# A hybrid decoder layer on one core: v of the last four heads in its own place, banks evacuated first, half of w_out split during attention

## The chip, the core and the metric

The kernel runs on one core of one Trainium2 chip. The core has five engines that work side by side, each through its own instructions in their order: TensorE (PE in the profile, PEld its weight loads), VectorE (DVE), ScalarE (ACT), GpSimd (POOL) and SyncE (SP), which here only issues DMAs. They wait for one another through semaphores. The metric is the device time of one launch in microseconds. Before the change the median of three runs was 2474.42 us (2474.41 to 2474.8).

## The reference

One layer over 2048 tokens of width 1024, in float32, with four RMS norms:

```
a   = RMSNorm(x)
mix = [ mLSTM, 4 heads || causal attention, 8 heads ](a) @ w_out
x   = x + RMSNorm(mix)
x   = x + RMSNorm( relu(RMSNorm(x) @ w_up)^2 @ w_down )
```

The input projection w_in gives q and k of the mLSTM (which go through a causal convolution of four taps and silu), its v, output gates and scalar gates, and two latents, c_q and c_kv, with one rotary key. The latents are normed and multiplied into q, k and v of the eight attention heads (64 plain and 32 rotary dimensions; v has 64). The mLSTM is computed in chunks with a carried state.

## The kernel before, in words

**Precision.** Nearly every operand is split in two: a high part rounded to the fast matmul type (ACT, a cast) and the low part that is left (DVE or POOL, a subtraction). A product is three matmuls, high by high, high by low, low by high: `mm3`, lines 220 to 222, the lines under which most matmuls stand in the profile.

**The order.** The instructions are not written in the order in which they run. Each step is handed to a planner (`Plan`, method `op`) with an engine, a cost in nanoseconds, the steps that it comes after, a key, the buffers ("rings") that it takes and those that it frees. `Plan.run` simulates the engines: on each it takes the step that can start first, and among those that can start at once the one with the smallest key; it calls the step, which emits its instructions, and so fixes the order on every engine. `kA(b, t)` = -400 + (123 b + t)/1.8 turns a place in block b of the projections into a key; in attention a key is a place in the sequence of score blocks, from 0 at the first. The chip then runs each engine's list in that order, and an instruction that is not ready holds back what stands behind it.

**Projections (four blocks of 512 tokens).** Per block: 16 units of 24 matmuls (`unit`, `values`), which accumulate in one of two PSUM banks, the ring "mm". A bank is free when its contents are evacuated: in `conv` by DVE into "raw" (L1051), in `gates` by DVE (L1131), in `values` by ACT into "vext" (L1104). From the latents come "kp", "vp", "qp" and "rp" (`operands`), in the same two banks; ACT copies the high part (`hi`, L727, L778), DVE the raw value (`raw`, L730, L781), POOL makes the low part. These evacuations have the key of their place, the products' 5 more (`PQ`). Beside them DVE runs the convolutions' taps (L1063), the rotation of the rotary key (`rotate`, L876 to 888, key `kA(b, KROT)`), the latents' gains (L675, key `kA(b, LGAIN)`), weight splits (L457) and the gates' scalar chain; `chunk` is the mLSTM (scores, exponentials, numerators L1186 and L1187, state, root, L1243 transposes, store "hT<-ho"). q, k and v of attention go to DRAM (qkd, qrd, krd, vd). In the last block the value units come at the end (`LASTLINE`).

**The switch to attention.** Memory is a stack on each side. On the left lie the convolutions' and latents' buffers (pool e2); on the right those of the chunks (b1, b2) and above them x and w (xp, wp). `switch1` closes e2; `switch2`, after the last unit, closes x and w and opens on the left the first operand set (QK[0]: q and k of one head, high and low, 97 rows by 4 by 2048) with the mask; `switch3`, after the last chunk, opens on the right v (16 tiles by 4 heads by 129 columns), the second operand set QK[1] and the buffers of attention. A tile's first write waits for the tiles whose memory it takes.

**Attention (8 heads, 4 query blocks each).** `maxima` finds each query's largest score ("m" products L1527, reductions on DVE into "mp" L1532 and L1534). `step` handles one block of 128 keys by up to 512 queries: three matmuls into S (three banks), two exponentials on ACT (L1591, L1595), the low part pl on DVE or, in one of five, on POOL (L1599), and the products with v into o (L1612, L1610, L1615). `out_rows` copies o away: ACT and DVE into "ot" (L1682, L1685), DVE into "ou" (L1689), POOL adds (L1692), SP stores "hT<-ot" (L1695) and the sums. "ot", "ou" and the two o banks have one buffer each. `load_v` (L1500) loads v for heads 0 to 3, and for heads 4 to 7 into the same tile, each pair of key tiles after its last product of head 3.

**Output projection and MLP.** `matrix(k)` loads 128 rows of w_out ("wor", ring "wr", two buffers), and ACT (L1822) and DVE (L1825) split two halves of them into tiles w0 to w11 or "wx". The pool `work` that holds these is opened by `left`, after all maxima and after head 6. `group` multiplies ("op") and adds the residual; the MLP follows with w_up and w_down in the same w tiles.

Of the kernel before, what the change touches and what calls it, by code (L numbers as in the profile page):

```python
# [10 lines left out]
F32 = mybir.dt.float32  # L11
# [28 lines left out]
EARLY = ()  # L40
LOL = 20.0
# [10 lines left out]
VLEAD = 0.0  # L52
# [9 lines left out]
CHUNK = 0.0  # L62
# [4 lines left out]
LGAIN = 30.0  # L67
# [3 lines left out]
KROT = 90.0  # L71
# [45 lines left out]
class Plan:  # L117
# [23 lines left out]
    def run(self):  # L141
# [70 lines left out]
def trunk(ctx: ExitStack, tc: tile.TileContext, x, xT, pos, wu, wout, wup, wdn, cols, rows, consts, edge, out, dbg=None):  # L212
# [486 lines left out]
    def operands(b, t, o_c, held):  # L699
# [25 lines left out]
        def two_parts(nm, n, q, last, first, key, store, kb):  # L725
# [36 lines left out]
        for n in range(4):  # L762
# [7 lines left out]
            def vevac(q, last, first, n=n, key=key):  # L770
# [16 lines left out]
                h = pl.op("Activation", 600, hi, [g, last], key + PQ, free=[("mm", first)])  # L787
                o_staged[b].append(g)
                d = pl.op("DVE", 690, raw, [g, last], key + PQ, free=[("mm", first)])
# [250 lines left out]
    def conv(b, j):  # L1040
# [36 lines left out]
        e = pl.op("DVE", 660, evac, [r, u["op"], o_rsbc[b]], key, free=[("mm", u["head"]), ("rsbc", o_rsbc[b])])  # L1077
# [11 lines left out]
    def values(b):  # L1089
# [3 lines left out]
        def one(c):  # L1093
# [22 lines left out]
            o_vx[b, c] = pl.op("Activation", 650, evac, [last, rs_x[b]["op"], *war], kA(b, TIME[b][5 + c] + 2), free=[("mm", head)])  # L1116
# [4 lines left out]
    def gates(b, h):  # L1121
# [9 lines left out]
        o = pl.op("DVE", 660, lambda: vec.tensor_tensor(g, u["p"], rsbc[b], ALU.mult), [u["op"], o_rsbc[b], *war], key, free=[("mm", u["head"]), ("rsbc", o_rsbc[b])])  # L1131
# [243 lines left out]
    a2 = av = ar2 = pq = pS = po = V = onecol = maskneg = maskb = identb = None  # L1375
# [9 lines left out]
    def switch1():  # L1385

        s_e.close()

    def switch2():

        nonlocal a2, maskneg, pq
        s_x.close()
# [4 lines left out]
        pq = pp(pc, "pq", 1)  # L1397
        pm.append(pp(pc, "pm", 2))

    def switch3():  # L1400

        nonlocal av, ar2, pS, po, V, maskb, identb, onecol
        s_b.close()
        av = sb(pa, "av", 1, "right")
# [8 lines left out]
        V = av.tile([P, NT, 4, 129], F32R, tag="V", name="V")  # L1413
# [4 lines left out]
    o_s1 = pl.op("X", 0, switch1, pl.groups["e2"], -KEYA)  # L1418
    o_s2 = pl.op("X", 0, switch2, unit_ops + [o_s1], -KEYA)
    o_s3 = pl.op("X", 0, switch3, pl.groups["in"] + [o_s2], -KEYA)  # L1420
    pl.group = "prep"
    for name, bufs, when in (
        ("q", 1, o_s2), ("m", 2, o_s2), ("S", SB_, o_s3), ("o0", 1, o_s3), ("o1", 1, o_s3), ("t", TB_, o_s3), ("th", 1, o_s3), ("tl", 1, o_s3), ("ph", HB_, o_s3), ("p", 1, o_s3), ("pl", LB_, o_s3), ("ot", 1, o_s3), ("ou", 1, o_s3),
        ("mp", 4, o_s2), ("mx", 2, o_s2), ("rsm", 2, o_s3),
    ):
        pl.ring(name, bufs, when)

    o_mask = pl.op("SP", 500, lambda: dma(maskneg, consts[:, K_MASK : K_MASK + 512]), [o_s2], key=-99, kb=256)
    o_const = {}
    for s in (0, "v", 1):  # L1430

        def fill(s=s):
            if s == "v":
                pool.memset(f32(V[:, :, :, 128:129]), 1.0)
# [7 lines left out]
        o_const[s] = pl.op("Pool" if s == "v" else "SP", 490 if s == "v" else 1500, fill, [o_s3 if s else o_s2], key=-99 if s == 0 else -50, kb=0 if s == "v" else 24)  # L1442
# [37 lines left out]
    def rotary_keys(s, b, key):  # L1480
        bs = slice(b * TB, (b + 1) * TB)
        o_kr[s, b] = pl.op("SP", 500, lambda: dma(f32(QK[s][64:96, 2:4, bs]), krd[:, :, bs]), [*o_krds[b], o_s3 if s else o_s2], key, kb=128)
# [1205 lines left out]
```

## Time and profile before

| | us |
|---|---|
| median of 3 runs | 2474.42 |
| the profiled execution | 2470.98 |
| its span, first to last instruction | 2469.2 |
| last matmul of a value unit | 539.2 |
| first product of attention with v ("o") | 564.4 |
| first product of the output projection ("op") | 1028.0 |

The span is the time from the first to the last instruction of that execution; 1.8 us of the execution lie outside it. The page gives the busy time of each engine; the granted clock says at what share of its full speed TensorE was let run (1.00 or, after idle stretches, 0.50), and a matmul at half clock counts as busy all the same. A row of the timeline gives the start, the duration, the engine, the line, the operation, the tile that is written and those that are read, and in brackets how long the engine had been idle and what ended that. A row of the waits gives the waiting engine, tile and line, whom it waited for, and total, number and longest of these waits. A row of the stages gives, per stretch, its length, busy time and number of instructions of PE, PEld, DVE, ACT and POOL, the granted clock, the DMA engines' busy share and the GB/s. SPq rows are DMAs being issued.

### The profile page before, as it was taken

To read this page: it belongs to the slowest core of one execution; us is meant where nothing else is said; L and a number is where in the kernel's file an instruction comes from. 1 tells how busy PE (TensorE), PEld (TensorE's weight loads), DVE (VectorE), ACT (ScalarE), POOL (GpSimd) and SP (SyncE) were. 2 spreads that over 40 slices of the span, in tenths; PEclk is the share of its full clock that TensorE was granted. 3 is DMA by queue.
4 is the path that set the end of the run, shared out by engine and by line. 5 is a ranking of instruction groups with operands and counts; after the bars stand their busy time and mean duration, and the time that the engine had idled before them with its cause. 6 is when DMAs were issued, how large, how long until landed. Compare 5 with 4: busy or idle time off the path is not lost.

```text
span 2469.2 us, 34097 instructions
## 1 busy us (share of the span) xinstructions
PE 2391.8 (97%) x10915; PEld 1920.1 (78%) x10915; DVE 1769.7 (72%) x3160; ACT 1359.8 (55%) x2638; POOL 811.1 (33%) x705
## 2 busy tenths in 40 slices
PE   8899999999999899999999999999999999999997
PEld 6677787677777677678888888888888888888885
DVE  6767565647887788754876677866676688786888
ACT  5545454436777777643666666756565343343454
POOL 3434333336878788522100000000000233232334
PEclk9999999999999999999999999999999999999999
DMA  6796969766325220466777798756664545445459
GB/s 239 231 331 212 342 220 334 225 194 143 69 57 109 66 53 10 136 194 226 258 213 218 227 284 249 218 160 194 195 194 141 165 136 165 136 138 167 131 164 244
DMA packets 345564, 456.02 MB, mean 185 GB/s; under 512 B 35324, under 2 KB 227848, under 8 KB 345384
## 3 DMA queue, kind: packets, MB, share of 16 engines
q1 hardware_dynamic: 341448, 446.98, 58.4%
q0 software_dynamic: 3936, 6.87, 1.7%
q8 instruction: 86, 1.41, 0.3%
q14 instruction: 94, 0.77, 0.1%
HBM read 302.79 MB, written 153.05 MB: 185 GB/s over the span
## 4 chain that ended last, share of the span: by engine, by line
PE 78%; DVE 7%; DMA 6%; issue 3%; POOL 2%; ACT 2%; SPq 1%; DVEq 0%; POOLq 0%; ACTq 0%
PE S L220 2%; PE o L1612 2%; PE mm L220 2%; PE o L1615 2%; PE S L221 2%; PE S L222 2%; PE mm L222 2%; PE mm L221 2%; PE m L1527 2%; PE op L220 1%; PE op L222 1%; PE op L221 1%; DMA hr<-hd 1%; PE mv L220 1%; PE mv L221 1%
## 5 line engine op out<-in xcount | busy, mean ns | idle before, releaser
L2499 POOL TENSOR_TENSOR y<-vd_0X,y 128x512 f32<-128x512 f32 x7 | 11.4, 1622 | 724.9 <-ACT vd_0X L2496 706.9
L1591 ACT ACTIVATE ph<-S 128x512 fp32r<-128x512 f32 (+1 forms) x320 | 170.2, 532 | 97.2 <-PE S L222 28.9
L1626 POOL TENSOR_TENSOR t<-t,ph 128x512 f32<-128x512 f32 (+1 forms) x192 | 210.3, 1096 | 16.5 <-ACT ph L1591 6.2
L2411 ACT CAST hh<-hr 128x512 fp32r<-128x512 f32 (+1 forms) x208 | 116.7, 567 | 168.2 <-DMA hr<-hd 37.3
L1599 DVE TENSOR_TENSOR pl<-S,ph 128x512 fp32r<-128x512 f32 (+3 forms) x272 | 157.0, 590 | 30.9 <-ACT S L1595 28.9
L220 PE MATMUL mm<-xh,wh 128*128 128x512 f32 x384 | 159.6, 416 | 11.5 <-ACT wh L452 7.7
L2416 DVE TENSOR_TENSOR hl<-hr,hh 128x512 fp32r<-128x512 f32 (+1 forms) x208 | 130.2, 635 | 36.6 <-ACT hh L2411 28.9
L221 PE MATMUL mm<-xl,wh 128*128 128x512 f32 x384 | 151.2, 394 | 2.7 <-DVE xl L382 2.7
L222 PE MATMUL mm<-xh,wl 128*128 128x512 f32 x384 | 151.2, 394 | 0.5 <-DVE wl L457 0.5
L1532 DVE TENSOR_REDUCE mp<-m 128x1 f32<-128x512 f32 x192 | 128.9, 682 | 29.3 <-PE m L1527 29.2
L1595 ACT ACTIVATE S<-S 128x512 f32<-128x512 f32 (+3 forms) x272 | 140.9, 518 | 0.3
L220 PE MATMUL S<-QK 97*128 97x512 f32 (+1 forms) x320 | 123.7, 386 | 5.9 <-DVE pl L1599 4.7
L1612 PE MATMUL o<-ph,V 128*128 128x512 f32 (+1 forms) x320 | 122.0, 382 | 7.5 <-DVE ot L1685 7.5
L221 PE MATMUL S<-QK 97*128 97x512 f32 (+1 forms) x320 | 118.6, 371 | 0.0
L1527 PE MATMUL m<-QK 96*128 96x512 f32 (+3 forms) x320 | 114.9, 405 | 3.4 <-DVE mp L1532 1.8
L222 PE MATMUL S<-QK 97*128 97x512 f32 (+1 forms) x320 | 118.1, 369 | 0.0
L1615 PE MATMUL o<-pl,V 128*65 128x512 f32 (+1 forms) x320 | 115.8, 364 | 1.2 <-DVE pl L1599 0.9
L2250 ACT ACTIVATE t<-t 128x512 f32<-128x512 f32 x96 | 60.6, 631 | 79.5 <-DVE t L2245 79.1
L220 PE MATMUL op<-wo,hh 128*128 128x512 f32 x256 | 101.9, 398 | 2.5 <-DVE x L1920 1.2
L222 PE MATMUL op<-wo,hl 128*128 128x512 f32 x256 | 100.5, 393 | 0.0
L221 PE MATMUL op<-wo,hh 128*128 128x512 f32 x256 | 100.5, 393 | 0.0
L220 PEld LDWEIGHTS mm<-xh,wh 128*128 128x128 f32 x384 | 73.0, 190 | 32.5 <-ACT wh L452 8.0
(6441 smaller groups left out, 7564.0 us busy)
## 6 DMA issues: line engine op xcount, KB each, us to landing
hr<-hd SPq DMA_DIRECT2D x100, 448.0 KB
wr<-in_wu_dram SPq DMA_DIRECT2D x71, 512.0 KB
hd<-t SPq DMA_DIRECT2D x128, 256.0 KB
hd<-ts SPq DMA_DIRECT2D x96, 256.0 KB
wl<-wparts SPq DMA_DIRECT2D x45, 512.0 KB
QK<-qkd SPq DMA_DIRECT2D x32, 512.0 KB
xt<-in_x_dram SPq DMA_DIRECT2D x28, 512.0 KB
xf<-xd SPq DMA_DIRECT2D x40, 256.0 KB
```

Source lines behind the costliest of these rows:

```text
L220: pe.matmul(o, ah, bh, start=start, stop=False)
L221: pe.matmul(o, ah, bl, start=False, stop=False)
L222: pe.matmul(o, al, bh, start=False, stop=stop)
L1527: pe.matmul(ps[:, :n], Qh[s][0:96, q0 : q0 + P], Kh[s][0:96, kb * TB : kb * TB + n], start=True, stop=True)
L1532: vec.tensor_reduce(mp["t"][:, j, kb : kb + 1], ps, axis=AX.X, op=ALU.max)
L1591: act.activation(t["h"][:, :w], t["S"][:, :w], AF.Exp)
L1595: act.activation(t["p"][:, :w], t["S"][:, :w], AF.Exp)
L1599: (pool if by_pool else vec).tensor_tensor(t["l"][:, :w], t["p"][:, :w], f32(t["h"][:, :w]), ALU.subtract)
L1612: pe.matmul(o0, v[:, 0:128], t["h"][:, :w], start=start, stop=stop)
L1615: pe.matmul(o1, v[:, 64:129], t["l"][:, :w], start=start, stop=stop)
L1626: pool.tensor_tensor(to, to, hv, ALU.add)
L2416: vec.tensor_tensor(t["l", m][:, :w], t["r", m][:, :w], f32(t["h", m][:, :w]), ALU.subtract)
```

## The change

Six things at once, all through the planner or the places of tiles:

- **Evacuations first.** `EV = 8` is taken from the keys of what frees an "mm" bank: the products' `hi` and `raw`, `conv`'s and `gates`' evacuation on DVE, `values`' on ACT. `PQ` goes from 5 to 0.
- **Other keys.** The rotation (`KROT` 90 to 50) and the latents' gains (`LGAIN` 30 to 20) come earlier, the chunks 2 later (`CHUNK`), v's loads 6 earlier (`VLEAD`).
- **First operand set at switch1.** QK[0], the mask and one maxima bank are opened when e2 closes, and their loads (mask, edge rows, rotary keys, q and k) are allowed from then on.
- **v twice.** `V[0]` (heads 0 to 3) is opened on the left by `switch2`, `V[1]` (heads 4 to 7) on the right by `switch3`; the loads of V[1] no longer wait for head 3.
- **w_out.** A pool work0 with the tiles w0 to w7 and "wr" is opened on the right by `switch3`. The first four of eight row blocks of w_out are loaded and split from then on, with keys at 0.6, 0.7, 0.8 and 0.9 of attention's length; the others as before.
- **"Z".** The steps that switch pools move from the planner's engine "X" to "Z", whose steps take effect at the end of what they follow, without the planner's latency. `EARLY` is empty, so the lines that would move maxima forward do nothing.

```diff
-VLEAD = 0.0
+VLEAD = 6.0
-CHUNK = 0.0
+CHUNK = 2.0
-LGAIN = 30.0
+LGAIN = 20.0
-KROT = 90.0
+KROT = 50.0
+W0 = 8
+W0K = 0.6
+W0S = 0.1
+EV = 8.0
-PQ = 5.0
+PQ = 0.0
...
-            if ops[d][0] == "X" or ops[d][0] == eng and eng != "SP":
+            if ops[d][0] in "XZ" or eng == "Z" or ops[d][0] == eng and eng != "SP":
...
-            h = pl.op("Activation", 570, hi, [g, last], key, free=[("mm", first)])
+            h = pl.op("Activation", 570, hi, [g, last], key - EV, free=[("mm", first)])
-            d = pl.op("DVE", 690, raw, [g, last], key, free=[("mm", first)])
+            d = pl.op("DVE", 690, raw, [g, last], key - EV, free=[("mm", first)])
...
-        e = pl.op("DVE", 660, evac, [r, u["op"], o_rsbc[b]], key, free=[("mm", u["head"]), ("rsbc", o_rsbc[b])])
+        e = pl.op("DVE", 660, evac, [r, u["op"], o_rsbc[b]], key - EV, free=[("mm", u["head"]), ("rsbc", o_rsbc[b])])
...
     def switch1():
 
+        nonlocal a2, maskneg, pq
         s_e.close()
-
-    def switch2():
-
-        nonlocal a2, maskneg, pq
-        s_x.close()
         a2 = sb(pc, "a2", 2)
         a1 = sb(pc, "a1", 1)
         set_tiles(a1, 0)
         maskneg = a1.tile([P, 512], F32, tag="maskneg", name="maskneg")
         pq = pp(pc, "pq", 1)
+
+    def switch2():
+
+        s_x.close()
         pm.append(pp(pc, "pm", 2))
+        V[0] = sb(pc, "a3", 1).tile([P, NT, 4, 129], F32R, tag="V0", name="V0")
 
     def switch3():
 
         s_b.close()
+        pools["work0"] = sb(ctx, "work0", 1, "right")
         av = sb(pa, "av", 1, "right")
...
-        V = av.tile([P, NT, 4, 129], F32R, tag="V", name="V")
+        V[1] = av.tile([P, NT, 4, 129], F32R, tag="V1", name="V1")
...
-        war = [o_pv[index[3, qb, kt]] for qb in range(NB) for kt in (t, t + 1) if (3, qb, kt) in index] if g else [o_const["v"]]
-        o_v[g, t] = [pl.op("SP", 1000, load, [o_vd[t], o_vd[t + 1], o_s3] + war, key, kb=512)]
+        o_v[g, t] = [pl.op("SP", 1000, load, [o_vd[t], o_vd[t + 1], *([o_s3, o_const["v"]] if g else [o_s2, o_const["v0"]])], key, kb=512)]
...
+    def wpool(ring):
+        return "work0" if int(ring[1:]) < W0 else "work" if int(ring[1:]) < WB else "w2"
...
     def wrow(name):
-        return pools["work"].tile([P, DM], F32, tag="wr", name=name, bufs=2)
+        return pools["work0"].tile([P, DM], F32, tag="wr", name=name, bufs=2)
...
-        key = END + 2 * k
-        a = pl.op("SP", 500, load, [o_left], key, take=("wr",), kb=512)
+        early = 2 * k + 1 < W0
+        key = END * (W0K + W0S * k) if early else END + 2 * k
+        a = pl.op("SP", 500, load, [o_s3 if early else o_left], key, take=("wr",), kb=512)
```

More of the change, by code (lines that the diff above doesn't have):

```diff
@@ L40 @@
 EARLY = ()
+EKEY = -165.0
+EGAP = 1.5
 LOL = 20.0
@@ L786, in vevac @@
                 g = pl.op("X", 0, place, [last], key + PQ, take=("sg",))
-                h = pl.op("Activation", 600, hi, [g, last], key + PQ, free=[("mm", first)])
+                h = pl.op("Activation", 600, hi, [g, last], key + PQ - EV, free=[("mm", first)])
                 o_staged[b].append(g)
-                d = pl.op("DVE", 690, raw, [g, last], key + PQ, free=[("mm", first)])
+                d = pl.op("DVE", 690, raw, [g, last], key + PQ - EV, free=[("mm", first)])
                 d = pl.op("Pool", 1300, lo, [h, d], key + PQ)
@@ L1115, in one @@
             war = o_chunk.get((b - 1, c), {}).get("v", [o_fill2])
-            o_vx[b, c] = pl.op("Activation", 650, evac, [last, rs_x[b]["op"], *war], kA(b, TIME[b][5 + c] + 2), free=[("mm", head)])
+            o_vx[b, c] = pl.op("Activation", 650, evac, [last, rs_x[b]["op"], *war], kA(b, TIME[b][5 + c] + 2) - EV, free=[("mm", head)])
         for c in range(4):
@@ L1130, in gates @@
         war = [x for c in range(4) for x in o_chunk.get((b - 1, c), {}).get("gate", [])]
-        o = pl.op("DVE", 660, lambda: vec.tensor_tensor(g, u["p"], rsbc[b], ALU.mult), [u["op"], o_rsbc[b], *war], key, free=[("mm", u["head"]), ("rsbc", o_rsbc[b])])
+        o = pl.op("DVE", 660, lambda: vec.tensor_tensor(g, u["p"], rsbc[b], ALU.mult), [u["op"], o_rsbc[b], *war], key - EV, free=[("mm", u["head"]), ("rsbc", o_rsbc[b])])
         o = pl.op("Activation", 590, lambda: act.activation(g, g, AF.Tanh, scale=0.5), [o], key)
@@ L1372, in trunk @@
             chunk(b, c)
-    a2 = av = ar2 = pq = pS = po = V = onecol = maskneg = maskb = identb = None
+    V = {}
+    pools = {}
+    a2 = av = ar2 = pq = pS = po = onecol = maskneg = maskb = identb = None
     pm = []
@@ L1433, in fill @@
             if s == "v":
-                pool.memset(f32(V[:, :, :, 128:129]), 1.0)
+                pool.memset(f32(V[1][:, :, :, 128:129]), 1.0)
                 pool.memset(f32(onecol[:, 0:64]), 0.0)
@@ L1440, in fill @@
                     pool.dma_start(z[s][96:97, :], edge[1:2])
[L1442 removed]
+        o_const[s] = pl.op("Pool" if s == "v" else "SP", 490 if s == "v" else 1500, fill, [o_s3 if s else o_s1], key=EKEY - 30 if s == 0 else -50, kb=0 if s == "v" else 24)
     blocks, first, start_of = [], {}, {}
@@ L1481, in rotary_keys @@
         bs = slice(b * TB, (b + 1) * TB)
-        o_kr[s, b] = pl.op("SP", 500, lambda: dma(f32(QK[s][64:96, 2:4, bs]), krd[:, :, bs]), [*o_krds[b], o_s3 if s else o_s2], key, kb=128)
+        o_kr[s, b] = pl.op("SP", 500, lambda: dma(f32(QK[s][64:96, 2:4, bs]), krd[:, :, bs]), [*o_krds[b], o_s3 if s else o_s1], key, kb=128)
     def load_qk(h, b, key):
@@ L1731, in trunk @@
         run += c
+    early = [x for x in EARLY for _ in range(4 * x[1] + 4)]
+    for i, x in enumerate(early):
+        keys[(*x, "m")][early[:i].count(x)] = EKEY + EGAP * i
     for s in range(2):
         for b in range(NB):
-            rotary_keys(s, b, -40 if s else -90 + b)
+            rotary_keys(s, b, -40 if s else EKEY - 30 + b)
     for h in range(NH):
@@ L1759, in trunk @@
     po1, po2, pA, pX, pB = (ExitStack() for _ in range(5))
-    pools = {}
     pl.group = "switch"
@@ L1768, in left @@
         pools["pmA"] = pp(pA, "pmA", 1)
-    o_left = pl.op("X", 0, left, pl.groups["prep"] + [o_pv[index[6, qb, kt]] for qb in range(NB) for kt in range(4 * qb + 4)], END)
+    o_left = pl.op("Z", 0, left, pl.groups["prep"] + [o_pv[index[6, qb, kt]] for qb in range(NB) for kt in range(4 * qb + 4)], END)
     for o in o_tail:
@@ L1775, in trunk @@
         pl.ring(name, bufs)
+    def wpool(ring):
+        return "work0" if int(ring[1:]) < W0 else "work" if int(ring[1:]) < WB else "w2"
     def wtile(name, ring):
-        where = "o1" if ring == "wx" else "work" if int(ring[1:]) < WB else "w2"
+        where = "o1" if ring == "wx" else wpool(ring)
         return pools[where].tile([P, 2, TB], F32R, tag=ring, name=name, bufs=4 if ring == "wx" else 1)
     def wrow(name):
-        return pools["work"].tile([P, DM], F32, tag="wr", name=name, bufs=2)
+        return pools["work0"].tile([P, DM], F32, tag="wr", name=name, bufs=2)
     def srow(name):
@@ L2105, in open_b @@
         pools["xb"] = sb(pX, "xb", 1, "right")
-    o_open = pl.op("X", 0, open_b, pl.groups["out"] + [o_openA], UP)
+    o_open = pl.op("Z", 0, open_b, pl.groups["out"] + [o_openA], UP)
     for z in ("Y0", "Y1", "Z0", "Z1"):
@@ L2528, in load @@
         def load():
-            q["x"] = pools["work" if int(ring[1:]) < WB else "w2"].tile([P, DM], F32, tag=ring, name=f"fx{ti}")
+            q["x"] = pools[wpool(ring)].tile([P, DM], F32, tag=ring, name=f"fx{ti}")
             dma(q["x"], x1d[ti * P : (ti + 1) * P, :])
```

29 lines of the change are left out of this document (15 added, 14 removed).

## The prediction

> **What bounds the kernel now.** I read the page first: shares of busy time and the chain that ended last.
>
> ```profile
> span 2469.2 us, 34097 instructions
> PE 2391.8 (97%) x10915; PEld 1920.1 (78%) x10915; DVE 1769.7 (72%) x3160; ACT 1359.8 (55%) x2638; POOL 811.1 (33%) x705
> PE 78%; DVE 7%; DMA 6%; issue 3%; POOL 2%; ACT 2%; SPq 1%; DVEq 0%; POOLq 0%; ACTq 0%
> ```
>
> TensorE is the bound. The change takes no matmul away, so it can win only two things: the 2469.2 - 2391.8 = 77.4 us in which PE was idle, and the time in which PE was busy at a low granted clock, which the 97% hides. So the second view was the table by stage, cut where the clock or PE's share changes (busy time and count of each engine, granted clock, DMA share, GB/s).
>
> ```profile
> 45.00:170.00 125.00, 113.96 (x511) 88.64 (x510) 95.93 (x167) 65.97 (x127) 52.68 (x46) 0.99 0.76 255
> 170.00:300.00 130.00, 126.99 (x594) 101.27 (x593) 84.25 (x173) 62.16 (x126) 52.74 (x48) 1.00 0.79 274
> ...
> 430.00:540.00 110.00, 103.43 (x459) 81.88 (x458) 62.69 (x137) 42.79 (x91) 41.38 (x42) 0.97 0.70 216
> 540.00:547.00 7.00, 4.17 (x24) 3.32 (x25) 4.13 (x15) 1.48 (x8) 2.02 (x4) 0.97 0.59 150
> 547.00:567.00 20.00, 18.58 (x56) 12.90 (x56) 14.44 (x41) 5.76 (x14) 3.05 (x7) 0.50 0.90 240
> ...
> 600.00:795.00 195.00, 192.43 (x988) 146.66 (x988) 158.86 (x365) 149.71 (x313) 158.72 (x138) 1.00 0.34 73
> 802.00:809.00 7.00, 0.43 (x3) 0.29 (x3) 1.68 (x3) 0.58 (x1) 0.30 (x2) 0.78 0.58 143
> 809.00:813.00 4.00, 4.00 (x12) 2.66 (x13) 2.24 (x7) 3.19 (x7) 3.48 (x4) 0.53 0.19 36
> 998.00:1028.00 30.00, 25.05 (x105) 17.08 (x104) 24.36 (x34) 23.99 (x51) 25.32 (x21) 0.94 0.35 93
> ...
> 1200.00:2400.00 1200.00, 1199.15 (x5312) 990.88 (x5311) 884.64 (x1353) 642.50 (x1157) 154.58 (x112) 1.00 0.61 185
> ```
>
> The MLP (1200 to 2400) has nothing to give. Four places have: the projections (45 to 540), the opening of attention (540 to 567), the reload of v (802 to 813) and the passage to the output projection (998 to 1028). The rest of attention is 98.7% busy. What PE waited for in the projections is in the view of waits (total us, times, longest):
>
> ```profile
> PE kp L220 <- DVE raw L1051: 3.6, 1, 3.6
> PE mm L220 <- ACT ks L727: 2.9, 4, 1.5
> ...
> PE mv L220 <- DVE raw L1051: 2.4, 1, 2.4
> ...
> PE mm L220 <- DVE ks L730: 0.3, 1, 0.3
> ```
>
> Thirteen rows of this kind, a product waiting for the evacuation of a "mm" bank (raw, ks, vs, gate, vext), add up to 15.6 us in 19 waits. How the longest arose, from the timelines of DVE and PE (start, duration):
>
> ```profile
> 456.72 1.68 DVE L879 TENSOR_TENSOR tg<-G,tg 32x512 f32<-32x512 f32 x1
> 458.43 2.32 DVE L1063 SCALAR_TENSOR_TENSOR cy<-raw,col,cy 128x512 f32<-128x512 f32 x3
> 460.67 0.69 DVE L1051 TENSOR_TENSOR raw<-mm,rsbc 128x512 f32<-128x512 f32 x1
> ```
>
> ```profile
> 461.41 0.79 PE L220 MATMUL kp<-ch,wh 128*128 128x512 f32 x1 [3.59 <-DVE raw L1051]
> ```
>
> DVE did a rotation and three taps of a convolution, for which PE was not waiting, and only then freed the bank.
>
> **Part 1, banks first (EV, PQ, KROT, LGAIN, CHUNK).** Nothing is added; the list scheduler sorts anew. In its keys the evacuation of convolution 3 in the last block stood at -400 + (369 + 38.4)/1.8 = -173.7, level with the taps; EV takes 8 off: -181.7, ahead of the taps and of the rotation (at KROT 50: -167.2). The products' evacuations move by 13 (PQ too). An engine does not stop an operation under way, so of 19 waits I keep about half a 0.69 us operation each: 19 x 0.35 = 6.6, and 15.6 - 6.6 = 9.0 is won. The clock of 0.97 over 110 us is 3.3 us of lost TensorE time beside such waits; I count half, 1.7. What steps back on DVE (taps, weight splits) is late next, at most 0.69 each; where PE needs it, some comes back: I take 1.7. Part 1: -9.0. Ends: -15.6 - 3.3 = -18.9 if every wait and drop goes; above zero if the displaced work bites (a rival below).
>
> **Part 2, v of the last heads in its own place.** The reload at 775 to 800 in one queue with the stores:
>
> ```profile
> 795.08 4.84 SPq L1500 DMA_DIRECT2D V<-vd  x4
> 800.64 2.30 SPq L1695 DMA_DIRECT2D hT<-ot  x1
> ```
>
> ```profile
> 800.64 6.68 DMA hT<-ot
> ```
>
> ```profile
> 808.84 0.76 PE L1612 MATMUL o<-ph,V 128*128 128x512 f32 x1 [6.57 <-DVE ot L1685]
> ```
>
> The store of one small query block queues behind v's loads and takes 6.68 us; "ot" has one buffer, so the next block's copy waits, the o banks stay full, and PE stands 6.57 us. Then the clock is 0.53 for 4 us: 0.47 x 4 = 1.9. With V1 apart the loads no longer wait for head 3, are not issued there, and both go: -8.5. Ends: 0 (the wait arises at another block) and -8.5.
>
> **Part 3, the opening.** What the move of the first operand set gives, I put at nothing:
>
> ```profile
> 522.13 0.60 SPq L1488 DMA_DIRECT2D QK<-qkd  x1
> ...
> 553.28 10.08 SPq L1500 DMA_DIRECT2D V<-vd  x12
> ...
> 577.14 0.50 SPq L1695 DMA_DIRECT2D hT<-ot  x1
> ```
>
> ```profile
> 538.78 0.39 PE L222 MATMUL mv<-wh,xl 128*128 128x512 f32 x1
> ...
> 564.39 0.63 PE L1612 MATMUL o<-ph,V 128*128 128x512 f32 x1
> ```
>
> ```profile
> 555.33 1.26 POOL L1599 TENSOR_TENSOR pl<-p,ph 128x512 fp32r<-128x512 f32 x1 [3.86 <-ACT p L1595]
> ```
>
> QK was being loaded at 522, before the last value product at 538.8: its place is the closed convolutions' already, whatever the planner's time says. It is v that comes late: its issue starts at 553.3, when the last chunk has given its memory back, and takes 10.08/12 = 0.84 us a transfer. V0 lies where x and w lay, free at 539.2, so its issue can start 14 us earlier. The first weights for it are ready at 555.33 + 1.26 = 556.6, so the first o, at 564.4, can come 7.8 us earlier. The half clock ended 2.6 us after that o; if its end moves along, 0.5 x 7.8 = 3.9 is won, and 1.1 of the 20 - 18.58 = 1.4 us of idle time: -5.0. The 2.8 us idle before 547 stay: PE waits there for the last chunk's normalisation. Ends: 0, and -(2.8 + 1.4 + 0.5 x 18.58) = -13.5.
>
> [...]
>
> New waits: V0's loads and its memset on POOL wait for the last value products. Behind them on SP stand the last chunk stores (read only by the output projection) and QK set 1; on POOL the last chunk's mask and root. And V1's sixteen transfers and two rows of w_out are free to go once the chunks end: 16 x 0.84 = 13.4 us of SP time, about where the first hT store was issued (577.1). V0's earlier start gives 14 us of it back, so I count +2.0; ends 0 and +8.5, the stall at 802 over again.
>
> **Part 4, half of w_out.**
>
> ```profile
> L1825 DVE TENSOR_TENSOR wo<-wor,wo 128x512 fp32r<-128x512 f32 x16 | 11.1, 719 | 7.9 <-ACT wo L1822 7.9
> ```
>
> ```profile
> L1822 ACT CAST wo<-wor 128x512 fp32r<-128x512 f32 x16 | 9.2, 618 | 8.2 <-DMA wor<-in_wout_dram 8.2
> ```
>
> ```profile
> PE S L220 <- DVE pl L1599: 3.6, 2, 1.8
> ```
>
> ```profile
> 1028.05 0.39 PE L220 MATMUL op<-wo,hh 128*128 128x512 f32 x1
> ```
>
> Eight of the sixteen pairs go into attention: 8 x 0.72 = 5.8 us on DVE and 8 x 0.62 = 5.0 on ACT. From 600 to 795 DVE is idle 36 us and ACT 45, and three S banks cover one delay; without them each split could cost its 0.72 on PE. I take +1.0, ends 0 and +5.8. In return the first op products need not wait until 1028: those of rows 0 to 3 read mLSTM outputs that have long been stored, so they can fill the 30 - 25.05 = 4.95 us of idle time (3.6 of it waits for pl) and spare some of 0.06 x 30 = 1.8 of clock. DVE is crowded there by hr and hl too, which stay: I take -4.0; ends -6.8 and 0.
>
> **The sum:** -9.0 - 8.5 - 5.0 + 2.0 + 1.0 - 4.0 = -23.5. The profiled execution took 2470.98 (span 2469.2 and 1.8 around it), so 2447.5 in its terms; the median of the runs is 3.4 above it: 2474.4 - 23.5 = 2450.9.
>
> **The rivals.** *A, waits change their names.* Part 1 gives nothing, since what stepped back (weight splits, xl, kw) is waited for instead. For it: from 45 to 170 DVE is busy 77%. Against: from 170 on 57 to 65%. 2450.9 + 9.0 = 2459.9. *B, the reload's stall moves to the opening*, because V1's loads stand ahead of the first small block's store: 8.5 instead of 2.0, 2457.4. A and B together: 2466.4. *C, the opening and the banks give more*: half of the way from each term to its end: 4.9 (part 1) and 4.3 (part 3), the 2.0 of the burst and 1.4 of part 4 besides: 12.6 less, 2438.3. *D, slower: evacuations push back what PE needs.* Per block DVE has 4 raw, 4 gate and 12 product evacuations, 80 in all; each put ahead costs the next DVE operation 0.69. If PE waits for that operation, the 15.6 come back as up to 55. The other parts give -14.5; for slower by over 4.9 us part 1 must cost +19.4, so (19.4 + 15.6)/0.69 = 51 of the 80 must hit PE; at 55 hits it is 2474.4 - 14.5 + 22.4 = 2482. DVE's idle time in the rows of the table speaks against it. *E, the clock does not follow v.* The stall before 547 sets the half clock off, and it runs out by itself at 567, whenever o begins; then part 3 wins only its 1.1 of idle time, and the time is 2450.9 + 3.9 = 2454.8. For it: PE was busy for nearly all of the 20 us, v or no v. Against: o began 2.6 us before the end, and after the stall at 802 the low clock fills the 4 us of its row, with o products running from 808.8.
>
> **How the numbers follow.** Forecast 0.40 (its own range 2444 to 2458), A 0.17, B 0.14, C 0.14, D 0.07, E 0.08. A measurement of this kernel can tell about 0.2%, 4.9 us, from no change. A with B ends 3 us from that bound, so 0.08 of their 0.31 goes to "same": faster 0.85, same 0.08, slower 0.07. The range reaches to C with some of its further end, and to A with B: 2433 to 2467; D and about half of C's tail are left out.
>
> **What would show it.** Right: of the bank waits in the projections a third left; no V loads near the fifth head's start and no wait over 1 us there; V loads issued from about 540 and the first o near 557, half clock until about 560; op products before the last head's end, no clock drop there. Wrong: bank waits at 15 us under other names (A), a wait of o for ot after the first query block (B), half clock still for 20 us though v is there (then the clock does not follow v), DVE waits of PE on cy, wl or xl that sum above 25 us (D).

## The result and the profile after

The changed kernel takes 2459.49 us (median of 4 runs, 2455.32 to 2460.7); the kernel before, run beside it, 2474.41 (2474.36 to 2474.8). The ratio is 0.9936 (95% interval 0.9919 to 0.9954): 14.9 us faster, where the prediction said 23.5. The profiled execution of the changed kernel took 2460.52 us. The first two lines below are the page's head, the third its chain.

```profile
span 2458.8 us, 34075 instructions
PE 2389.0 (97%) x10915; PEld 1916.9 (78%) x10915; DVE 1767.7 (72%) x3160; ACT 1357.7 (55%) x2638; POOL 825.1 (34%) x706
PE 83%; DVE 6%; DMA 5%; ACT 2%; issue 2%; POOL 1%; SPq 1%; DVEq 0%; ACTq 0%; POOLq 0%
```

TensorE was idle for 77.4 us before and is idle for 2458.8 - 2389.0 = 69.8 now. The same stretches as in the prediction's table by stage (length, busy time and count of PE, PEld, DVE, ACT, POOL, granted clock, DMA share, GB/s):

```profile
45.00:170.00 125.00, 112.01 (x497) 87.97 (x495) 94.15 (x166) 61.98 (x124) 55.54 (x45) 0.96 0.71 231
170.00:300.00 130.00, 123.90 (x572) 98.08 (x572) 85.32 (x173) 62.73 (x126) 53.01 (x49) 1.00 0.80 275
...
430.00:540.00 110.00, 105.45 (x483) 82.98 (x481) 63.75 (x138) 42.36 (x86) 42.47 (x41) 1.00 0.78 251
540.00:547.00 7.00, 4.50 (x15) 3.75 (x16) 5.03 (x14) 1.69 (x7) 3.09 (x5) 0.67 1.08 289
547.00:567.00 20.00, 18.25 (x60) 12.65 (x59) 14.94 (x43) 6.20 (x20) 4.12 (x8) 0.59 0.89 226
...
802.00:809.00 7.00, 6.36 (x31) 4.07 (x29) 6.28 (x16) 4.63 (x11) 6.41 (x7) 1.00 0.11 22
809.00:813.00 4.00, 4.00 (x21) 3.04 (x21) 3.00 (x7) 3.04 (x7) 2.76 (x3) 1.00 0.11 33
998.00:1028.00 30.00, 27.07 (x122) 19.94 (x121) 27.46 (x36) 21.83 (x47) 23.12 (x17) 1.00 0.36 98
```

The reload (802 to 813) and the passage to the output projection (998 to 1028) are healed. The stretch from 45 to 300 us has become worse (TensorE 2.0 and 3.1 us less busy, the clock 0.96 for 0.99 in its first part), the end of the projections better, and the opening of attention (540 to 567) is no better.

Where the time went is read most safely from the *offset*: PE executes the same matmuls of each kind in both kernels, so the n-th of a kind is looked up in both traces and the starts are subtracted. A matmul is named by the tile that it writes: "mv" belongs to a value unit, "ht" to the transposes at the end of a chunk, "o" to attention, "op" to the output projection. After minus before, in the two profiled executions:

| matmul | offset, us | the step that it closes |
|---|---|---|
| 200th "mv" (in block 2, at 336 us) | +7.1 | projections, blocks 0 and 1 |
| last "mv" (538 us) | -0.7 | projections, blocks 2 and 3: -7.8 |
| first "o" (565 us) | +1.1 | opening: +1.8 |
| 367th "o" (785 us) | +3.5 | first four heads: +2.4 |
| 401st "o" (806 us) | -4.7 | reload: -8.1 |
| 701st "o" (981 us) | -5.4 | last four heads: -0.8 |
| 267th "op" (1083 us) | -14.0 | passage: -8.5 |
| last "op" (1204 us) | -13.9 | |
| end of the span | -10.4 | MLP and tail: +3.5 |

The last row is not put down to the change. From the last "op" to the end the profiled execution of before took 1250.9 us; the changed kernel took 1254.4, and the twelve kernels below, one of which is the kernel before in that part (1253.4), 1252.6 to 1256.2. The profiled execution of before was quick there, and 3.4 us under its own median.

### The profile page after: what moved, and what is told of

The parts are those of the page before. It is cut to its first block, busy times and chain, and to the rows that moved or that the text cites. A ratio compares the mean times of both kernels' runs of the same rounds, so it can differ in the third digit from the quotient of the medians.

```text
span 2458.8 us, 34075 instructions
## 1 busy us (share of the span) xinstructions
PE 2389.0 (97%) x10915; PEld 1916.9 (78%) x10915; DVE 1767.7 (72%) x3160; ACT 1357.7 (55%) x2638; POOL 825.1 (34%) x706
## 4 chain that ended last, share of the span: by engine, by line
PE 83%; DVE 6%; DMA 5%; ACT 2%; issue 2%; POOL 1%; SPq 1%; DVEq 0%; ACTq 0%; POOLq 0%
PE mm L226 3%; PE mm L227 3%; PE mm L228 3%; PE S L226 3%; PE o L1622 3%; PE S L227 2%; PE S L228 2%; PE o L1625 2%; PE m L1537 2%; PE op L226 2%; PE op L227 2%; PE op L228 2%; PE mv L227 1%; PE mv L226 1%; PE mv L228 1%
```

## The experiments

Each kernel is the changed one with the edit shown, unless it says otherwise. Times are medians; the kernel before took 2473.33 to 2473.69 beside them. They are grouped by part here; where a text speaks of the second or the eleventh experiment, it counts in the order in which they ran: 1 all keys back, 2 head 0's loads back, 3 no early half of w_out, 4 the planner's wait, 5 v held back by data, 6 both edits together, 7 stores from ACT's queue, 8 the evacuations' keys back, 9 the other keys back, 10 two buffers, 11 evacuations first in blocks 2 and 3, 12 the best version.

### The keys of the first part

**All keys back** (five constants, in one line here).

```diff
-CHUNK, LGAIN, KROT, EV, PQ = 2.0, 20.0, 50.0, 8.0, 0.0
+CHUNK, LGAIN, KROT, EV, PQ = 0.0, 30.0, 90.0, 0.0, 5.0
```

> The changed kernel with its evacuation keys, rotary keys and chunk key put back as they were before; the places of v, the opening's loads and w_out stay changed. Theory: the keys move 7 us of loss into blocks 0 and 1 and 8 us of gain into blocks 2 and 3, so with the old keys block 1 ends 7 us earlier than in the changed kernel (within 1 us of the kernel before), the last projection matmul is where it was to within 1.5 us (538 to 540 us), and the time stays within 2 us of the changed kernel's 2459.5. Rival, as the prediction had it: the keys are worth 9 us, the last projection matmul moves from 538 to about 547 us, and the time is about 2468.

Measured: 2462.98 us (2462.29 to 2463.7), ratio 0.9961 (0.9947 to 0.9975); 200th "mv" 7.0 us earlier than in the changed kernel, last "mv" 1.7 later. The matmuls did what the theory says; the time lies between its range (within 2 us of 2459.5) and the rival's 2468.

**The evacuations' keys alone back.**

```diff
-EV, PQ = 8.0, 0.0
+EV, PQ = 0.0, 5.0
```

> The changed kernel with the evacuations' keys alone put back (EV 0, PQ 5); the rotary keys, the gains' lead and the chunk key stay as changed. With all keys back blocks 0 and 1 were 7.0 us faster, and blocks 2 and 3 lost 8.7 us again. Theory: the loss in block 0 is the evacuations' (they go ahead of the taps, and the splits of the weights come after the taps), so with their keys back block 1 ends 4 to 7 us earlier than in the changed kernel; the gain in blocks 2 and 3 is that of the evacuations as well, and goes: the last projection matmul at 538 to 541 us. Rival: the rotary keys and the chunk key make both the loss and the gain; then every offset up to 540 us stays within 2 us of the changed kernel.

Measured: 2482.28 us (2477.84 to 2485.05), 1.0029 (1.0017 to 1.0041): slower than before. The loss of the early blocks did not go (200th "mv" 1.5 us later still), so the expectation failed in its first half; the last "mv" came 17.3 us later.

**The other keys alone back.**

```diff
-CHUNK, LGAIN, KROT = 2.0, 20.0, 50.0
+CHUNK, LGAIN, KROT = 0.0, 30.0, 90.0
```

> The changed kernel with the evacuations ahead of other work (EV 8, PQ 0), but the other keys of the first part back as before (KROT 90, LGAIN 30, CHUNK 0). All keys back (first experiment) ended block 1 7.0 us earlier and the projections 1.7 us later than the changed kernel; the evacuations' keys alone back (eighth) ended block 1 1.0 us later and the projections 17.3 us later. Theory, that the two groups act apart: the other keys cost 8 us in blocks 0 and 1 and more in block 3, the evacuations gain; then with EV alone block 1 ends 6 to 9 us earlier than in the changed kernel, the last projection matmul is 5 to 15 us earlier (523 to 533 us), and the time is 2445 to 2455. Rival: the groups only work together, since the other keys bring forward what the evacuations push back; then the projections end where the changed kernel's do or later, 538 to 548 us, and the time is 2459 to 2469, although block 1 may end earlier.

Measured: 2454.79 us (2453.27 to 2456.2), 0.9918 (0.9902 to 0.9935), so inside the theory's range, but not by its mechanism: the last "mv" was at 537.17, only 0.9 earlier, and the 200th where it was (-0.1). The groups do not act apart. Each alone costs the early blocks what both cost; without the evacuations first, the other keys also cost 7.9 us from block 2 on (219.2 for 211.3 in the table below). With them first, moving the other keys wins nothing there (203.5 for 202.4). The rest of this kernel's gain came at the first "o", 24.9 us after the last "mv" for 27.4.

**Evacuations first in blocks 2 and 3 alone**, on top of that.

```diff
-EV = 8.0
+EVB = (0.0, 0.0, 8.0, 8.0)
-PQ = 0.0
+PQB = (5.0, 5.0, 0.0, 0.0)
```

`EVB[b]` and `PQB[b]` then stand where `EV` and `PQ` stood.

> The ninth experiment's kernel (rotary keys, gains' lead and chunk key as before), with the evacuations ahead of other work in blocks 2 and 3 alone; blocks 0 and 1 have the old keys. Theory: the first part's loss and gain are the same keys in other blocks. With all keys old block 1 ends 7.0 us earlier than in the changed kernel and blocks 2 and 3 lose 8.7 us; with the evacuations first everywhere block 1 ends as in the changed kernel and blocks 2 and 3 lose nothing more. So block 1 ends about 7 us earlier, the last projection matmul is at 529 to 533 us against 537.2 in the ninth, and the time is 2446 to 2451 (2454.8 less 4 to 8). Rival: the early blocks' order is what the late blocks live on (what is evacuated late in block 1 is still open when block 2 begins), so blocks 2 and 3 lose the 7 us again and the time stays at 2453 to 2457; or block 1 does not win at all.

Measured: 2450.87 us (2449.62 to 2452.6), 0.991 (0.9896 to 0.9923); 200th "mv" 5.3 us earlier than in the changed kernel, last "mv" at 532.69. The theory holds. One profile of such an offset is not worth much by itself, though: kernels whose projections are the same differ by up to 4 us at their end. All fourteen profiles together (in the last row first this kernel, then the last one below):

| keys | profiles | first "mv" of block 2, us | from there to the last "mv", us |
|---|---|---|---|
| old | 3 | 327.8 to 329.6, mean 328.4 | 211.0 to 211.9, mean 211.3 |
| as changed | 7 | 331.7 to 334.9, mean 333.3 | 202.8 to 204.5, mean 203.5 |
| evacuations first everywhere, others old | 1 | 334.8 | 202.4 |
| evacuations old, others as changed | 1 | 336.2 | 219.2 |
| evacuations first in blocks 2 and 3, others old | 2 | 329.6 and 327.4 | 203.1 and 205.4 |

So the first part costs 4.8 us up to block 2 and wins 7.8 from there, 2.9 in all, and all of the loss can be left off. Why it costs is seen in the waits of PE in the changed kernel, 45 to 540 us (total, times, longest), of which these are the largest:

```profile
PE mv L227 <- DVE wl L463: 5.2, 2, 3.0
PE mm L226 <- ACT vs L784: 3.3, 1, 3.3
PE mm L226 <- ACT ks L733: 3.0, 5, 1.3
```

The wait for "raw" shrank from 6.0 us to 1.3, but the rows for banks still add up to 14.5 (15.6 before), and the splits of the weights, 0.6 before, now cost 5.9. In block 0 DVE evacuates "raw" 5.4 us earlier than before (55.43 for 60.85) and splits later (timeline of DVE, changed kernel):

```profile
59.77 2.18 DVE L463 TENSOR_TENSOR wl<-wr,wh 128x1024 fp32r<-128x1024 f32 x1
61.87 3.61 DVE L1069 SCALAR_TENSOR_TENSOR cy<-raw,col,cy 128x512 f32<-128x512 f32 x3
65.40 1.22 DVE L463 TENSOR_TENSOR wl<-wr,wh 128x1024 fp32r<-128x1024 f32 x1
```

The 3.3 us are not work put ahead on DVE. DVE and ACT could not begin, for want of a staging tile whose store ("qkd<-ks") had not landed, and half clock lasted from 126.0 to 132.8 us (timelines of DVE, ACT and PE):

```profile
125.79 0.69 DVE L787 COPY vs<-vp 128x512 f32<-128x512 f32 x1 [1.24 <-DMA qkd<-ks]
126.52 0.59 ACT L784 CAST vs<-vp 128x512 fp32r<-128x512 f32 x1 [2.16 <-DVE vs L787]
127.16 0.80 PE L226 MATMUL mm<-xh,wh 128*128 128x512 f32 x1 [3.25 <-ACT vs L784]
```

This stall goes with the other keys (rotation, gains, chunks), not with the evacuations first. At this matmul PE waited 2.7 to 3.8 us in the seven profiles with both groups changed, 5.7 with the other keys alone, 0.8 with the evacuations first alone, and 0.3 in the five with old keys in this block. Which of the other keys makes the store late was not tried.

With the old keys in blocks 0 and 1 no wait for vs is over 0.5 us, and the splits cost 2.1 (waits of PE in the kernel with evacuations first in blocks 2 and 3, 45 to 540 us):

```profile
PE mm L226 <- ACT ks L733: 3.3, 5, 1.5
...
PE mv L226 <- DVE raw L1057: 2.4, 1, 2.4
PE mv L227 <- DVE wl L463: 2.1, 1, 2.1
```

### The opening

**Head 0's loads back at the last projection's place**, v's own place kept.

```diff
-    o_mask = pl.op("SP", 500, lambda: dma(maskneg, consts[:, K_MASK : K_MASK + 512]), [o_s1], key=EKEY - 30, kb=256)
+    o_mask = pl.op("SP", 500, lambda: dma(maskneg, consts[:, K_MASK : K_MASK + 512]), [o_s2], key=-99, kb=256)
```

The edge rows, the rotary keys (key -90 + b) and `load_qk` change in the same way.

> The changed kernel, but head 0's q and k loads, its rotary keys and the mask wait for the last projection's place again, as in the kernel before; v's own place stays. Theory: those loads stand on SP's queue ahead of the last chunk's E (issued at 531.66 us instead of 525.60), and this holds back the last ht from 546.8 to 554.3 us; without them in front E goes at about 525, the last ht ends by 548, and the first o is at 557 to 561 us instead of 565.5: the time is 4 to 8 us under the changed kernel, 2452 to 2456. Rival 1: q and k are then late instead, first m and first S wait for them, and the opening gives the same time to within 1.5 us or loses up to 4 us (2458 to 2464). Rival 2: the opening is set by the half clock between 547 and 567 us and not by any load; first o moves by less than 1.5 us.

Measured: 2465.06 us (2463.28 to 2469.26), 0.997 (0.9961 to 0.998). The positions of the theory came true and its time did not; the first rival's loss is there, and 1 us larger than its range. Positions, counted from the last "mv" (E is the last chunk's table of exponents, loaded from DRAM):

| kernel | E issued | last "ht" | v's first load | first "o" | 101st "o" |
|---|---|---|---|---|---|
| before | -13.2 | 8.7 | 14.5 | 25.6 | 86.4 |
| changed | -6.4 | 16.9 | -1.1 | 27.4 | 89.9 |
| this one | -12.2 | 9.8 | -0.2 | 25.0 | 96.5 |
| this one, v of the last heads held back | -12.2 | 9.8 | -0.2 | 23.5 | 86.8 |
| all keys back | -12.9 | 12.1 | -1.0 | 22.3 | 89.0 |
| evacuations first in blocks 2 and 3 | -6.9 | 12.5 | -2.7 | 23.2 | 85.3 |

In the changed kernel q and k, the mask and the rotary keys stand in SP's queue from 512 us, and the DMA engines' busy share from 530 to 538 us is 1.03, 0.53 before; the last chunk's E is issued behind them, 6.1 us later than before, and then takes 6.78 us. ACT waits, and with it the chunk's exponentials, numerators and transposes (from the chain, ACT's and PE's timelines of the changed kernel):

```profile
531.66 6.78 DMA E<-wd
```

```profile
538.46 1.27 ACT L1172 ACTIVATE E<-E,tm 128x128 f32<-128x128 f32 x4 [8.95 <-DMA E<-wd]
```

```profile
554.32 1.11 PE L1249 MATMUL ht<-cst,hn 128*128 128x128 f32 x4
...
565.46 0.63 PE L1622 MATMUL o<-ph,V 128*128 128x512 f32 x1
```

In all nine profiles with head 0's loads first, the first "o" follows the last "ht" by 10.0 to 10.6 us, with "ht" anywhere from 12.1 to 16.9: the opening hangs on the last chunk. With the loads last "ht" comes 7 us earlier, and the first "o" only 2.4: in this kernel's chain the maxima of head 0 ("m" products and their reductions on DVE) now stand between the two, up to 553 us. From 581 us on that was lost again (ACT's timeline of this kernel):

```profile
584.17 0.58 ACT L1692 COPY ot<-o 64x512 f32<-64x512 f32 x1 [4.62 <-DMA hT<-ot]
```

It is the stall of 802 us over again: the first block's store, issued at 578.76, stands behind ten loads of v for the last heads and takes 5.38 us. In the changed kernel the copy came later, at 584.89, and did not wait.

**The planner's wait for head 3 put back**, v in two places.

```diff
+        war = [o_pv[index[3, qb, kt]] for qb in range(NB) for kt in (t, t + 1) if (3, qb, kt) in index] if g else []
-        o_v[g, t] = [pl.op("SP", 1000, load, [o_vd[t], o_vd[t + 1], *([o_s3, o_const["v"]] if g else [o_s2, o_const["v0"]])], key, kb=512)]
+        o_v[g, t] = [pl.op("SP", 1000, load, [o_vd[t], o_vd[t + 1], *war, *([o_s3, o_const["v"]] if g else [o_s2, o_const["v0"]])], key, kb=512)]
```

> The changed kernel; v of the last four heads keeps its own place, but each of its loads waits again for head 3's products with the same tiles of v. Theory: the stall at 800 us came from that wait alone, so it returns: o of head 4 waits for v again, PE loses 8 us between 800 and 812 us, and the half clock behind it comes back; the opening, where the 16 loads no longer stand on SP between 571 and 588 us, wins 0 to 2 us. 2465 to 2468. Rival: the stall came from the size of one burst on one queue or from the drop of the clock at the change of heads, which a place of its own does not change; then the time stays at 2458 to 2461 with the waits' order alone changed.

Measured: 2458.41 us (2454.32 to 2459.68), 0.9941 (0.9926 to 0.9956). The experiment did not do what it was meant to: a dependency that only the planner knows makes no wait on the chip. The loads went at 587 to 611 us instead of 571 to 588, and decide nothing about the reload.

**v of the last heads held back by data.** GpSimd writes sums from the finished rows (two per partition) into each pair of v's tiles, which the load then overwrites; the load comes after that step, `o_gv[t]`.

```diff
+            def gate():
+                pool.tensor_tensor(V[1][0:64, g0 : g0 + 2, 0, 0], t["t"][0:64, 0:2], t["u"][0:64, 0:2], ALU.add)
+
+            o_gv[g0] = pl.op("Pool", 200, gate, [a, o_const["v"]], key - 3, free=[("ot", o_ot)])
```

> The changed kernel; the 16 loads of v for the last four heads are held back by data: GpSimd writes two elements of each pair of v's tiles from the finished rows of heads 1 and 2 (eight small additions in all), and the load of that pair overwrites them, so they go two at a time between about 630 and 750 us and not in one burst at 571 to 588 us. Theory: the burst costs the opening what the kernel with the planner's wait won by moving it to 587 to 611 us (2.5 us at the 33rd product, given back at 606 to 628 us when the loads came there); spread out, 2 to 3 us stay won, and nothing is lost at 800 us: 2455 to 2458. Rival 1: in the changed kernel as it stands the burst hides behind PE's half clock, and nothing is won (within 1.5 us of 2459.5). Rival 2: each pair of loads now stands on SP's queue in front of a block's store, as at 800 us in the kernel before, and costs PE 1 us or more eight times: 2465 or more.

Measured: 2465.7 us (2460.86 to 2467.79), 0.9961 (0.9946 to 0.9977). The second rival, though in two places and not eight: 5.4 us were lost between 667 and 687 us, 2.1 between 727 and 748. At the first, DVE's reciprocal of the sums waits for a load behind a pair of v's, and PE for what stands behind the reciprocal on DVE (timelines of DVE and PE); the granted clock is 0.86 from 665 to 690 us, 1.00 in the changed kernel:

```profile
672.12 0.18 DVE L1713 RECIPROCAL rsm<-rsm 128x4 f32<-128x4 f32 x1 [2.94 <-DMA rsm<-sumd]
```

```profile
672.95 0.80 PE L226 MATMUL S<-QK 97*128 97x512 f32 x1 [2.13 <-DVE pl L1609]
```

Up to the 101st "o" nothing was won: it comes 91.0 us after the last "mv", against 89.9 in the changed kernel. So in the changed kernel itself the burst cost the opening nothing that shows, as the first rival has it.

**Both edits together.**

> The loads of head 0 back at the last projection's place, as in the second experiment, and v's loads for the last four heads held back as in the fifth. The second experiment showed the last ht 7 us earlier and the first o 2.4 us earlier against the projections' end, and then lost 6.5 us between 581 and 628 us, where ScalarE's copy of the rows waited 4.62 us for the store hT<-ot that was queued behind 14 loads of v. Theory: the store's wait is the burst's; without it the opening keeps the 2.4 us and loses nothing at 581 us, so against the projections' end it is 2 to 5 us better than the changed kernel, and 7 to 9 us better than the second experiment: 2454 to 2458. Rival: DMA as a whole is what fills the opening (its share is 1.10 to 1.17 between 538 and 580 us), and the wait changes its name: q and k of head 1 are late instead, and the time is that of the second experiment to within 2 us (2463 to 2467).

Measured: 2461.76 us (2459.39 to 2466.18), 0.9954 (0.9938 to 0.9971). Up to the 101st "o" it is 3.1 us better than the changed kernel and 9.7 better than the second experiment (table above): most of that stall was the burst of v's loads. A shorter wait is left: at 579.74 us PE stands 2.10 us for "ot". The held back pairs then cost 7.3 us at the two places of the fifth experiment, and the time lies between the theory's range and the rival's.

**Head 0's loads back, two buffers for rows and sums.**

```diff
-("ot", 1, o_s3), ("ou", 1, o_s3)
+("ot", 2, o_s3), ("ou", 2, o_s3)
```

> The second experiment's kernel (head 0's loads at the last projection's place), with two buffers each for a block's rows and sums (ot and ou), 4 KB more per partition: a store that is late then holds nothing back. Theory: the 6.5 us that the second experiment lost between 581 and 628 us came from the copy of the rows waiting 4.62 us for a store behind v's loads, and from the clock after it; with a second buffer 4 to 6 us of them stay, the first o stays 2.4 us earlier against the projections' end than in the changed kernel, and the time is 2455 to 2460 (the second experiment's 2465.1 less 5 to 10). Rival: what stands behind the store is late all the same (the sums' way back through DMA, q and k of heads 1 and 2 in the same queue), another wait takes its place within 10 us, and the time stays at 2462 to 2466.

Measured: 2463.49 us (2459.06 to 2464.65), 0.9952 (0.9937 to 0.9968): the rival. The store no longer holds anything, and 10 us later the two loads behind the burst do (timelines of DVE and ACT):

```profile
594.74 0.18 DVE L1713 RECIPROCAL rsm<-rsm 128x4 f32<-128x4 f32 x1 [3.88 <-DMA rsm<-sumd]
```

```profile
593.32 0.62 ACT L1838 CAST wo<-wor 128x512 fp32r<-128x512 f32 x1 [3.13 <-DMA wor<-in_wout_dram]
```

The second row is the fourth part's: an early half of w_out.

### The reload and w_out

**The kernel before, stores of rows and sums from ACT's DMA queue**, v in one place and waiting for head 3.

```diff
-            dma(hT[512 + h * 64 : 576 + h * 64, bs], t["t"][0:64])
-            dma(sumd[h : h + 1, bs], t["u"][64:65])
+            act.dma_start(hT[512 + h * 64 : 576 + h * 64, bs], t["t"][0:64])
+            act.dma_start(sumd[h : h + 1, bs], t["u"][64:65])
```

> The kernel before with one edit: the stores of each finished block of attention (its rows and its sums) are issued from ScalarE's DMA queue and not from SP's. Theory: the stall at 800 us is a store that is queued behind v's loads on SP (6.68 us for hT<-ot, ScalarE's copy waiting 7.19 us for it); in a queue of its own the store lands in about 2 us, PE's 6.57 us at 802 to 809 us and most of the half clock behind it go, v staying in one place with its wait on head 3: 6 to 8 us faster than before at the products of head 4, less what 64 issues cost ScalarE (0 to 4 us in all attention). 2466 to 2470. Rival: the products of head 4 wait for v's tiles themselves, which can't be loaded ahead of head 3's last products; then PE's stall stays within 1.5 us and only what it waits for changes, 2473 to 2477.

Measured: 2474.31 us (2470.3 to 2482.75), 1.0008 (0.9996 to 1.002). The time lies in the rival's range; the profiled execution is the slowest of ten, 2482.75. The mechanism is shown in its first half: between the 367th and the 401st "o" the kernel wins 6.8 us on the kernel before. PE's wait before the 397th "o", 6.57 us before, is 1.36 here. But a second wait follows it, and then half clock for 6.83 us from 815.4, as long as before (waits of PE from 785 to 830 us and table by stage of this kernel):

```profile
PE m L1527 <- DVE mp L1532: 1.4, 1, 1.4
PE o L1612 <- DVE ot L1685: 1.4, 1, 1.4
```

```profile
805.00:815.00 10.00, 7.10 (x36) 4.71 (x34) 6.57 (x16) 6.08 (x15) 7.59 (x8) 1.00 0.86 188
815.00:819.00 4.00, 3.95 (x12) 2.75 (x12) 3.08 (x6) 1.21 (x3) 2.41 (x2) 0.55 0.09 20
```

So 4.1 of the 6.8 us go again by the 434th "o" (the sums' load, still on SP, takes 4.52 us at 809). The first four heads lose 6.3 us besides; that this is the price of the 32 more issues on ACT is not shown.

**No early half of w_out.**

```diff
-W0 = 8
+W0 = 0
```

> The changed kernel with no part of w_out loaded before attention is left (the tiles are placed as before, and all sixteen halves wait for the last head). Theory: the early half is worth what the offsets of the same matmuls show between 990 and 1083 us, 8.4 us, of which little is lost again: the first op goes from 999 to about 1025 us, and the time is 2466 to 2469. Rival, as the prediction had it: 4 us less 1 us in attention, so 2462 to 2463. Second rival: the gain is given back behind it, since half of what the offsets win up to 1083 us is lost by the end; 2460 to 2463, with the offset at 1083 us at +8 and the one at the end at +4 or less.

Measured: 2468.68 us (2463.3 to 2471.72), 0.9983 (0.9974 to 0.9993); first "op" at 1025.03, offset +0.5 at the 701st "o" and +9.2 at the 267th "op", kept to the end. The theory holds: 8.7 us between the two.

```profile
998.00:1028.00 30.00, 23.62 (x93) 16.66 (x92) 25.36 (x34) 20.48 (x46) 21.99 (x17) 0.89 0.27 76
```

Without the early half PE is busy 23.62 of 30 us at 0.89, with it 27.07 at 1.00.

### The best version

The kernel with the evacuations first in blocks 2 and 3 and two buffers for "ot" and "ou".

> The eleventh experiment's kernel with two buffers for a block's rows and sums, as in the tenth. Theory: in the tenth the products gained 3.6 us from the 100th to the last (offset +1.6 to -1.9 us against the changed kernel), since a late store holds nothing back in any head; the opening stays as in the eleventh or wins up to 1 us. So 2 to 4 us less than the eleventh, 2443 to 2448. Rival: those 3.6 us were given back by a worse order in the opening and are no gain of the second buffer; then it is within 1.5 us of the eleventh.

Measured: 2447.34 us (2446.03 to 2449.3), 0.9895 (0.9882 to 0.9909): faster than both kernels, its interval clear of the changed kernel's. The theory holds: 3.5 us less than the eleventh. From the first to the last "o" of attention it wins 4.5 us on the eleventh; its first "o" is 1.7 later.

## Why the prediction was right or wrong, point by point

- **Part 1 (-9.0): mis-sized.** It measured -2.9 over all profiles, and 3.5 by the medians with and without the keys (the intervals of the two ratios overlap). The step that failed is "of 19 waits I keep about half a 0.69 us operation each": the bank waits fell from 15.6 us to 14.5. One of them was no order of DVE's (3.3 us for the staging tile), and "what steps back on DVE (taps, weight splits) is late next, at most 0.69 each" was wrong in block 0, where three taps of 3.61 us stand ahead of the split that PE waits for. In blocks 2 and 3 7.8 us were won, but not by the term's mechanism alone: from 300 to 540 us the bank waits fell only from 7.1 us to 4.9. Two stretches of half clock, 6.83 us at 461 and 482, are gone, which is worth 3.4 and was counted as 1.7; what the rest is was not traced. Rival A described the early blocks, with the split of the weights by name.
- **Part 2 (-8.5): right**, -8.1 at the place, by the mechanism that the prediction gave; the stores' own queue cuts the same stall from 6.57 us to 1.36.
- **Part 3 (-5.0, burst +2.0): wrong.** The step is "what the move of the first operand set gives, I put at nothing". It costs the last chunk 8.2 us ("ht" at 16.9 for 8.7 after the last "mv"), because its loads stand ahead of E (with them late again it is 9.8); the changed kernel's opening came out 1.8 us longer, not 5.0 shorter. The step "the first o can come 7.8 us earlier" falls too: with v early and head 0's loads late it is 0.6 earlier than before, as head 0's maxima are the next bound. That the clock's end follows v, as 3.9 of the 5.0 us assume, is not shown either: the half clock ended 2.6 us after the first "o" before, 4.3 after it in the changed kernel, and 1.9 ahead of it with both edits together. The +2.0 for the burst is not what cost the changed kernel: without the burst it was no faster up to the 101st "o". Rival B is what the second experiment ran into; in the changed kernel, opening and first four heads together lost 4.2 where -2.0 was forecast (-5.0 + 2.0 + 1.0). Of these, 2.4 lie in the first four heads, and where they come from stays open.
- **Part 4 (+1.0, -4.0): the mechanism right, the +1.0 not there, the -4.0 right at its place and short as a whole.** The splits cost nothing that shows in the last four heads (they won 0.8), and in the first they are late only behind the burst; the passage gave -8.5, beyond the end of -6.8, and 8.7 with the early half alone taken out. That end was the idle time and the clock of one window, 998 to 1028 us. Of the 8.5, 4.1 stand from the 61st to the 130th "op" (up to 1048 us), which is the forecast. Another 1.1 come by the 151st and 2.9 between 1080 and 1083, which the window left out. They are not clearly the early half's: without it the kernel wins 1.1 and 1.9 at the same two places, after being 3.8 us slower than before at the 130th "op". Why it is slower there was not traced.
- **The sum.** -2.9 + 4.2 - 8.1 - 0.8 - 8.5 = -16.1, against -14.9 between the medians. Against the forecast the first part gave 6.1 less, the opening with the first heads 6.2 less, and the passage 4.5 more. The measured 2459.5 lies inside the wide range, 2433 to 2467, and just outside the forecast's own, 2444 to 2458. That it is rival A's 2459.9 is luck: only the first of the three is A's mechanism, and the other two nearly cancel.
- **Open:** why the other keys cost 7.9 us from block 2 on without the evacuations first was not tried.

## What to carry to other kernels

A key that puts one kind of work first must be asked per stage what it puts second: here the same keys cost 4.8 us in two blocks and won 7.8 in two others, and giving them to the latter alone kept the gain. A load that is allowed earlier takes its place in the queue from something (here E was issued 6.1 us later, and ACT stood 8.95 us for it); before putting it "at nothing", list what is issued on that queue in the stretch that it moves into, and who waits for it. In SP's queue the burst of v's loads was moved, not removed: its price showed at whichever small transfer stood behind it (a store, for which ACT stood 4.62 us, the sums' way back, DVE 3.88, a weight row, ACT 3.13), so look at the issue list around each.

## What the runs showed of the hardware

In the profiles before and after the granted clock is 1.00 or 0.50. In the opening, half clock lasted 20.48 us in the kernel before, 6.83 and 17.07 in the changed kernel and 10.24 with both edits together, all multiples of 3.41. Divided at that length, the row of 547 to 567 reads (kernel before):

```profile
546.50:549.90 3.40, 2.65 (x8) 1.55 (x8) 3.14 (x12) 0.00 (x0) 0.97 (x2) 0.51 0.48 121
549.90:553.30 3.40, 3.09 (x11) 2.31 (x11) 3.11 (x10) 1.08 (x3) 0.81 (x5) 0.50 0.82 227
553.30:556.80 3.50, 3.50 (x13) 2.51 (x11) 0.99 (x3) 1.89 (x4) 1.26 (x1) 0.50 0.89 237
556.80:560.20 3.40, 2.85 (x11) 2.01 (x10) 3.12 (x9) 1.18 (x5) 0.00 (x0) 0.50 1.12 298
560.20:563.60 3.40, 3.31 (x11) 2.21 (x12) 3.11 (x8) 0.58 (x1) 0.00 (x0) 0.50 1.13 296
563.60:567.00 3.40, 3.40 (x10) 2.52 (x9) 1.48 (x5) 1.03 (x2) 0.00 (x0) 0.50 1.00 259
```

PE had no gap in the third and the sixth of these rows, and the full clock came back behind the sixth. Divided in the same way, the half clock of the changed kernel from 552.7 us has PE at 3.13, 2.98, 3.40, 3.40 and 3.40 of 3.40 us, that with both edits together at 2.69, 2.89 and 3.40, and that with all keys back, from 549.9 us, at 2.82, 3.00, 3.50 of 3.50 and 3.40. So in these four the last row before the full clock has no gap. No rule follows from it: four rows without a gap (the third above, two in the changed kernel, one with all keys back) were followed by more half clock, and at 461.2 us in the kernel before, PE was busy 3.22 of 3.41 us, and the full clock followed. The ends of matmuls are modelled in these records, so small gaps are uncertain. Rival E, a half clock that runs out by itself, is not what the traces show: in the opening it lasted 10.24 us with both edits together and 20.48 in the kernel before. What ends it was not shown. What counts for a kernel is that a gap can cost more than its own length: PE's wait of 3.59 us up to 461.4 us in the kernel before was followed by half clock to 464.6, and its wait of 6.57 us up to 808.8 by half clock to 812.8.
